# Weight tiles split once per layer and kept in DRAM, the normalised rows of the half that is used again kept there too, and six buffers of weight pairs

## The chip, the cores and the metric

The kernel runs on one core of one Trainium2 chip. Its metric is the device time of one launch in microseconds. Five engines work side by side, each through its own queue in order: TensorE (PE; its weight loads are PEld), VectorE (DVE), ScalarE (ACT), GpSimd (POOL) and SyncE (SP). SP only issues DMAs, and all of the kernel's own DMAs are issued there.

## The reference

An encoder trunk of two layers over two sequences of 1024 rows by 1024 columns, all in float32. Cut to what matters here, a layer is:

```
mod = silu(c) @ w_ada + b_ada;  shift, scale, gate = split(mod)
h    = rms_norm(x, g_pre) * (1 + scale) + shift
proj = h @ w_in                                  # 1024 x 4024, laid out as 32 tiles of 128 columns
mixed = concat(attention, rwkv7, mamba2, gated_deltanet)(proj)   # groups A, B, C, D, 256 wide each
x    = x + gate * rms_norm(mixed @ w_out, g_post)
```

Both sequences use the same `w_in` and `w_out` in a layer. Columns of `proj` feed the four head groups; B and D hold a scan in each direction, C a chunked scan, A an attention over all 1024 rows.

## The kernel before

A unit is one sequence in one layer; there are four, in the order (layer 0, sequence 0), (0, 1), (1, 0), (1, 1). Work on a unit has three parts: the input projection, the mixers, the output projection.

**Precision by splitting.** A projection multiplies float32 operands as pairs: `a = ah + al`, where `ah` is a rounded copy in the matmul's fast format and `al` the rest, and it sums `ah·bh`, `al·bh` and `ah·bl`. Rows `h` are held as `hh`, `hl`, weights as `wh`, `wl`. `split_w` makes a weight pair out of a loaded tile `w` of 128x512: ACT casts (line 327), DVE subtracts (line 329). Both are marked urgent, so the scheduler puts them ahead of the mixers' work on their queues.

**Input projection.** `stage_in` works on one half of a sequence, 512 rows, at a time. `norm_in` (lines 274 to 299) loads the rows, normalises them, transposes them on PE (line 294) and writes `hh` and `hl`; there is one buffer of each, 2 MB each. `in_tile` then goes through the weight tiles: two loads of 256 KB, two splits, 24 matmuls 128x512 through `paced` (line 458), one copy out of PSUM, one store to the tensor `P` in DRAM. The tiles for groups D and C of both halves come first, then the rest, so that a half is visited again after the other has overwritten `hh` and `hl`, and `norm_in` runs again on it: on both halves in unit 0, on the first half in the others. `norm_in` runs 13 times in all: four in unit 0, three in each other unit. A weight tile is loaded and split again for each half of each unit, 512 times for `w_in` and 128 times for `w_out` (`out_tiles`).

**Order.** A scheduler places every instruction by priority and simulated time. `spread`, `behind` and `ahead` give projection tiles priorities that are spread over the mixers' stretch, so that the projections' matmuls fill PE beside the scans; `paced` chains every few of them (TK, TO) through a memset of a token on POOL (line 462), which keeps them from running away. Buffers order the rest: `w` has two, `wh` and `wl` three each (GB, GL), the copy out of PSUM (`st`) three.

Of the kernel before, what the change touches and what calls it, by code (L numbers as in the profile page):

```python
# [10 lines left out]
F32 = mybir.dt.float32  # L11
F32R = mybir.dt.float32r
# [7 lines left out]
MUL, ADD, SUB = ALU.mult, ALU.add, ALU.subtract  # L20
# [1 line left out]
D = 1024  # L22
MIX = 1800
EA = 60
GK = 4
GB = 3
EB = 60
TK = 5
TO = 8
ED = 90  # L30
GL = 3
SB = 3
NPT = 8
EC = 60
T = 1024
DEPTH = 2
# [10 lines left out]
NWT = len(W_TILES)  # L47
W_D = ['sm', 'qkv0', 'qkv1', 'qkv2', 'qkv3', 'qkv4', 'qkv5']
W_B = ['xbc0', 'xbc1', 'xbc2', 'xbc3', 'xbc4', 'xbc5']
W_REST = ['zc0', 'zc1', 'zd0', 'zd1', 'wa', 'rkv0', 'rkv2', 'rkv4', 'rkv1', 'rkv3', 'rkv5', 'cq0', 'cq1', 'cq2', 'ckv', 'zb0', 'zb1', 'za0', 'za1']  # L50
W_ORDER = W_D + W_B + W_REST
# [57 lines left out]
class Body:  # L109
    def __init__(self, ctx, tc, A, outs, sl=None):  # L110
        self.tc, self.nc, self.A, self.outs = tc, tc.nc, A, outs
        self.n = 0
        self.side = "left"
        self.span = None
        nc = tc.nc
        self.cp = ctx.enter_context(tc.tile_pool(name="cp", bufs=1))
        self.dr = ctx.enter_context(tc.tile_pool(name="dr", bufs=1, space=DRAM))
        self.banks = 3
        self.held = None
        self.token = self.t(self.cp, [1, 1], tag="token")  # L120
        self.gate, self.run = None, 0
        self.ident = self.const(self.cp, "ident")
        self.blk = self.const(self.cp, "blk")
        self.bsel = self.const(self.cp, "bsel")
        self.cc = self.t(self.cp, [128, 4], tag="cc")
        nc.vector.memset(self.cc[:, 0:1], -0.5)
        nc.vector.memset(self.cc[:, 1:2], EPS)
        nc.vector.memset(self.cc[:, 2:3], 0.5)
        nc.vector.memset(self.cc[:, 3:4], 1.0)
        self.mhalf, self.eps, self.phalf, self.one1 = (self.cc[:, i:i + 1] for i in range(4))  # L130
# [127 lines left out]
                    for j in range(2):  # L258
                        nc.vector.tensor_scalar(L.gsc[:, k0 + j, :], ps2[:, 2 * j:2 * j + 2], 1.0, L.pp("gpre", k0 + j), ADD, MUL)

    def stage_in(self, s, L, l, xsrc, Pd, parts=((0, W_ORDER), (1, W_ORDER))):

        for hf, names in parts:
            if self.held is None or self.held[0] != (Pd, hf):
                self.spread()
                hh = self.t(self.pj, [128, 8, 512], F32R, tag="hh")
                hl = self.t(self.pj, [128, 8, 512], F32R, tag="hl")
                self.norm_in(s, L, xsrc, hf, hh, hl)
                self.held = (Pd, hf), hh, hl
            for name in names:  # L270
                self.spread()
                self.in_tile(l, name, hf, *self.held[1:], Pd)

    def norm_in(self, s, L, xsrc, hf, hh, hl):
            nc, pj, sp = self.nc, self.pj, self.sp
# [25 lines left out]
    def in_tile(self, l, name, hf, hh, hl, Pd):  # L301
        nc, pj = self.nc, self.pj
        ci = W_TILES.index(name)
        M = 88 if name == "sm" else 128
        ps = self.t(self.pps, [128, 512], tag="pj")
        for k in range(8):
            if k % 4 == 0:
                w = self.t(pj, [128, 4, 128], tag="w", bufs=2)
                self.dma(w, self.A["w_in"][l, ci][:, k * 128:k * 128 + 512].rearrange("p (k c) -> p k c", k=4))
            if k % GK == 0:  # L310
                with self.urgent():
                    wh, wl = self.split_w(w[:, k % 4:k % 4 + GK], [128, GK, 128])
            for i, (a, b) in enumerate(((wh, hh), (wh, hl), (wl, hh))):
                self.paced(TK, ps[0:M], a[:, k % GK, 0:M], b[:, k, :], dict(start=(k == 0 and i == 0), stop=(k == 7 and i == 2)))
        st = self.t(pj, [128, 512], tag="st", bufs=SB)
        with self.urgent():
            if name[0] == "z":
                nc.scalar.activation(st, ps, AF.Tanh, scale=0.5)
                nc.vector.scalar_tensor_tensor(st, st, 1.0, ps, ADD, MUL)
            else:  # L320
                nc.scalar.copy(st[0:M], ps[0:M])
        self.dma(Pd[ci * 128:ci * 128 + M, hf * 512:(hf + 1) * 512], st[0:M])

    def split_w(self, w, shape):
        nc, pj = self.nc, self.pj
        wh = self.t(pj, shape, F32R, tag="wh", bufs=GB)
        nc.scalar.copy(wh, w)  # L327
        wl = self.t(pj, shape, F32R, tag="wl", bufs=GL)
        nc.vector.tensor_tensor(wl, w, wh.bitcast(F32), SUB)  # L329
        return wh, wl  # L330

    def out_tiles(self, l, ch, hh, hl, kqs, at=lambda kq: kq):

        nc, pj = self.nc, self.pj
        pss = [self.t(self.pps, [128, 2, 256], tag="pj") for _ in range(2)]
        for n, kq in enumerate(kqs):
            w = self.t(pj, [128, 2, 256], tag="w", bufs=2)
            self.dma(w, self.A["w_out"][l, ch, kq // 2][:, (kq % 2) * 512:(kq % 2) * 512 + 512].rearrange("p (k c) -> p k c", k=2))
            with self.urgent():
                wh, wl = self.split_w(w, [128, 2, 256])  # L340
            for i in range(4):
                ps = pss[i // 2][:, i % 2]
                c = slice(i * 128, (i + 1) * 128)
                for k in range(2):
                    a, b = hh[:, at(kq) * 2 + k, c], hl[:, at(kq) * 2 + k, c]
                    first, last = n == 0 and k == 0 and i % 2 == 0, n == len(kqs) - 1 and k == 1
                    for m, (u, w2) in enumerate(((a, wh), (a, wl), (b, wh))):
                        self.paced(TO, ps, u, w2[:, k], dict(start=first and m == 0, stop=last and m == 2, skip_group_check=True))
        return pss

    def stage_out(self, s, L, l, xsrc, od, dst):
# [3 lines left out]
        for hf in range(2):  # L355
# [1249 lines left out]
    def full(self):  # L1605
        A = self.A
        x = [A["x0"], A["x1"]]
        L = [self.layer_params(l) for l in range(DEPTH)]
        P = {}
# [4 lines left out]
        def src(s, l):  # L1614
            return x[s] if l == 0 else x1[s]

        def run_in(u, *parts):
            s, l = units[u]
            if u not in P:
                P[u] = self.t(self.dr, [NWT * 128, 1024], tag="P", bufs=2)  # L1620
            self.stage_in(s, L[l], l, src(s, l), P[u], parts)

        def run_out(u):
            s, l = units[u]
# [20 lines left out]
        def out_last(parts, ctx=None):  # L1645
            s, l = units[3]
            self.stage_out_last(s, L[l], l, src(s, l), o[3], self.outs[s], parts, ctx)

        early = (0, W_D + W_B), (1, W_D + W_B)
        late = (1, W_REST), (0, W_REST)  # L1650
        with ExitStack() as io:
# [62 lines left out]

# [12 lines left out]
```

## Time and profile before

| | before |
|---|---|
| median of three runs | 4856.7 us (4849.28 to 4880.52) |
| the profiled execution's own time | 4863.89 us |
| its span | 4862.1 us |
| PE / PEld / DVE / ACT / POOL busy | 89% / 67% / 69% / 45% / 8% |
| mean granted TensorE clock | 0.877 |
| moved by DMA | 671.79 MB, 138 GB/s |

The profile is of one execution. Busy time counts an engine's instructions, not its waits; a wait is put down to the instruction that ended it. The chain of waits goes back from the last instruction to what released it, and its shares add up to the span.

### The profile page before, as it was taken

To read this page: it belongs to the slowest core of one execution; us is meant where nothing else is said; L and a number is where in the kernel's file an instruction comes from. 1 tells how busy PE (TensorE), PEld (TensorE's weight loads), DVE (VectorE), ACT (ScalarE), POOL (GpSimd) and SP (SyncE) were. 2 spreads that over 40 slices of the span, in tenths; PEclk is the share of its full clock that TensorE was granted. 3 is DMA by queue.
4 is the path that set the end of the run, shared out by engine and by line. 5 is a ranking of instruction groups with operands and counts; after the bars stand their busy time and mean duration, and the time that the engine had idled before them with its cause. 6 is when DMAs were issued, how large, how long until landed. Compare 5 with 4: busy or idle time off the path is not lost.

```text
span 4862.1 us, 100716 instructions
## 1 busy us (share of the span) xinstructions
PE 4303.3 (89%) x38644; PEld 3243.0 (67%) x38644; DVE 3351.1 (69%) x6837; ACT 2177.4 (45%) x4734; POOL 399.5 (8%) x2093
## 2 busy tenths in 40 slices
PE   6879798999898988998989898898989988889985
PEld 3657565767676775764767666775767766767675
DVE  2488878567688886555549869767556969857466
ACT  2444364554435453531554454454445254446233
POOL 0111010000101110000011100000011100000000
PEclk8889898998998897988989799797989988878688
DMA  4444364343543455453445354644245345365233
GB/s 146 136 146 143 99 196 145 100 114 117 164 148 121 144 162 158 129 152 100 138 144 164 113 166 132 197 140 135 70 149 177 129 135 157 111 200 146 75 100 127
DMA packets 495063, 671.79 MB, mean 138 GB/s; under 512 B 149752, under 2 KB 265976, under 8 KB 493560
## 3 DMA queue, kind: packets, MB, share of 16 engines
q1 hardware_dynamic: 494584, 665.36, 43.9%
q8 instruction: 306, 5.01, 0.4%
q14 instruction: 173, 1.42, 0.1%
HBM read 486.53 MB, written 178.57 MB: 137 GB/s over the span
## 4 chain that ended last, share of the span: by engine, by line
PE 58%; DVE 16%; DMA 14%; issue 5%; ACT 5%; SPq 1%; POOL 1%; DVEq 0%; POOLq 0%; ACTq 0%
PE pj L458 27%; PE b L824 2%; DVE iA L522 2%; PE b L1570 2%; PE b L551 2%; DMA w<-w_in 2%; PE pj L243 2%; PE b L557 1%; PE b L1557 1%; DVE wl L329 1%; DVE GT L537 1%; SPq L144 1%; PE y L1222 1%; PE b L1526 1%; PE b L590 1%
## 5 line engine op out<-in xcount | busy, mean ns | idle before, releaser
L458 PE MATMUL pj<-hh,wl 128*128 128x512 f32 (+1 forms) x2048 | 849.4, 415 | 41.9 <-DVE wl L329 28.8
L458 PE MATMUL pj<-hh,wh 128*128 128x512 f32 (+1 forms) x2048 | 854.2, 418 | 25.8 <-POOL token L462 10.2
L458 PE MATMUL pj<-hl,wh 128*128 128x512 f32 (+1 forms) x2048 | 847.4, 414 | 18.3 <-POOL token L462 18.2
L327 ACT CAST wh<-w 128x512 fp32r<-128x512 f32 x640 | 395.6, 618 | 782.6 <-PE pj L458 523.8
L329 DVE TENSOR_TENSOR wl<-w,wh 128x512 fp32r<-128x512 f32 x640 | 447.3, 700 | 253.3 <-ACT wh L327 211.7
L458 PEld LDWEIGHTS pj<-hh,wl 128*128 128x128 f32 (+1 forms) x2048 | 397.2, 194 | 148.1 <-DVE wl L329 27.6
L458 PEld LDWEIGHTS pj<-hh,wh 128*128 128x128 f32 (+1 forms) x2048 | 398.0, 194 | 128.8 <-POOL token L462 16.1
L458 PEld LDWEIGHTS pj<-hl,wh 128*128 128x128 f32 (+1 forms) x2048 | 397.8, 194 | 113.9 <-POOL token L462 26.3
L462 POOL MEMSET token<- 1x1 f32 x1613 | 143.4, 89 | 3347.0 <-PE pj L458 3342.1
L458 PE MATMUL pj<-wh,hl 128*128 128x256 f32 x896 | 270.7, 313 | 1.3 <-DVE hl L363 1.2
L1561 ACT ACTIVATE pT<-b 128x512 f32<-128x512 f32 x256 | 150.7, 598 | 262.7 <-PE b L1559 258.2
L458 PE MATMUL pj<-wh,hh 128*128 128x256 f32 x768 | 236.2, 308 | 11.5 <-ACT st L372 5.9
L458 PE MATMUL pj<-wl,hh 128*128 128x256 f32 x768 | 231.5, 302 | 3.7 <-DVE wl L329 3.7
L294 PE MATMUL pj<-c_ident,x 128*128 128x128 f32 x416 | 120.4, 393 | 122.0 <-DVE x L289 43.9
L1527 DVE TENSOR_REDUCE mx<-b 128x1 f32<-128x512 f32 x256 | 169.9, 684 | 84.1 <-PE b L1526 82.4
L638 DVE SCALAR_TENSOR_TENSOR cva<-cvi,cw,cva 128x1024 f32<-128x1024 f32 x144 | 183.7, 1278 | 46.8 <-ACT cva L634 33.8
L458 PEld LDWEIGHTS pj<-wh,hl 128*128 128x128 f32 x896 | 182.8, 208 | 17.5 <-issue 9.7
L1570 PEld LDWEIGHTS b<-VO,pT 128*64 128x64 f32 x4096 | 152.8, 144 | 52.1 <-issue 43.9
L1570 PE MATMUL b<-VO,pT 128*64 128x65 f32 x4096 | 182.5, 233 | 0.9 <-ACT pT L1561 0.9
L824 PE MATMUL b<-AR,BK 64*64 64x128 f32 x2048 | 178.4, 305 | 3.5 <-DVE G L829 3.2
L829 DVE SCALAR_TENSOR_TENSOR G<-b,Dk,mk 128x128 f32<-128x128 f32 x512 | 140.7, 341 | 53.2 <-PE b L824 52.8
L296 ACT ACTIVATE ht<-pj,shc,gsc 128x256 f32<-128x256 f32 x208 | 118.6, 570 | 126.8 <-PE pj L294 63.2
(403 smaller groups left out, 9125.1 us busy)
## 6 DMA issues: line engine op xcount, KB each, us to landing
w<-w_in SPq DMA_DIRECT2D x512, 256.0 KB
P<-st SPq DMA_DIRECT2D x248, 256.0 KB
x<-x SPq DMA_DIRECT2D x76, 512.0 KB
w<-w_out SPq DMA_DIRECT2D x128, 256.0 KB
G<-P SPq DMA_DIRECT2D x112, 256.5 KB
cvi<-P SPq DMA_DIRECT2D x48, 512.0 KB
f<-acr SPq DMA_DIRECT2D x32, 512.0 KB
bkc<-bkd SPq DMA_DIRECT2D x64, 256.0 KB
```

The lines of the kernel that those rows point to most:

```text
L294: nc.tensor.transpose(ps[:, i * 128:(i + 1) * 128], xs[i][:, k * 128:(k + 1) * 128], self.ident)
L296: nc.scalar.activation(ht, ps[:, 0:256], AF.Identity, scale=L.gsc[:, k, s:s + 1], bias=L.shc[:, k, s:s + 1])
L327: nc.scalar.copy(wh, w)
L329: nc.vector.tensor_tensor(wl, w, wh.bitcast(F32), SUB)
L458: m = self.nc.tensor.matmul(*mm[:3], **mm[3]).ins
L462: t = self.nc.gpsimd.memset(self.token, 0.0).ins
L638: nc.vector.scalar_tensor_tensor(a, c[:, j:j + 1024], wt(j, i), a, MUL, ADD)
L824: nc.tensor.matmul(pss[x][self.half(x ^ a), i * 128:i * 128 + 128], BK[self.half(x), pr, c, a], AR[self.half(x), pr, c].rearrange("p a t - ...
L829: v.scalar_tensor_tensor(G[:, x, pr, c, :], pss[x][:, i * 128:i * 128 + 128], Dk[:, c, 2 * x + pr:2 * x + pr + 1], mk, MUL, MUL)
L1527: v.tensor_reduce(mx[:, n, qt:qt + 1], ps, AX.X, ALU.max, negate=True)
L1561: nc.scalar.activation(pT[kt], ps, AF.Exp)
L1570: nc.tensor.matmul(po[64 * x:64 * x + 64, i, :], pT[kt][:, o:o + 64], VO[:, kt, h, :], start=(kt == 0 and i == 0), stop=(kt == 7), skip_gr ...
```

## The change

`split_w` gives way to `halves`. On the first use of a tile in a layer it loads `w`, splits it into the two halves of one 4 KB wide buffer `w2`, and stores the pair, 512 KB, into a tensor in DRAM. On each later use of the same tile (the other half, the other sequence) it loads the pair from there, 512 KB, and splits nothing. `w2` has six buffers; `wh` and `wl` are gone. The first `norm_in` of a half that will be visited again (five of them, the set `twice`) also stores `hh` and `hl`, 2 MB each, and the second visit loads them in place of running `norm_in`. The setting `dynamic_dma_scratch_size` goes from its default to 1024.

```diff
 def stage_in(...):
...
-                self.norm_in(s, L, xsrc, hf, hh, hl)
+                back = self.spilled.get((s, l, hf))
+                if back is None:
+                    self.norm_in(s, L, xsrc, hf, hh, hl)
+                    if again[n]:
+                        self.spilled[s, l, hf] = back = self.t(self.dr, [2, 128, 4096], tag="hd", bufs=2)
+                        for i, h in enumerate((hh, hl)):
+                            self.dma(back[i], h.bitcast(F32).rearrange("p k t -> p (k t)"))
+                else:
+                    for i, h in enumerate((hh, hl)):
+                        self.dma(h.bitcast(F32).rearrange("p k t -> p (k t)"), back[i])
...
 def in_tile(...):
-                w = self.t(pj, [128, 4, 128], tag="w", bufs=2)
-                self.dma(w, self.A["w_in"][l, ci][:, k * 128:k * 128 + 512].rearrange("p (k c) -> p k c", k=4))
-            if k % GK == 0:
-                with self.urgent():
-                    wh, wl = self.split_w(w[:, k % 4:k % 4 + GK], [128, GK, 128])
+                w2 = self.halves(("in", l, ci, k // 4), lambda: self.A["w_in"][l, ci][:, k * 128:k * 128 + 512]).rearrange("p u (k c) -> p u k c", k=4)
...
-    def split_w(self, w, shape):
+    def halves(self, key, src):
+
         nc, pj = self.nc, self.pj
-        wh = self.t(pj, shape, F32R, tag="wh", bufs=GB)
-        nc.scalar.copy(wh, w)
-        wl = self.t(pj, shape, F32R, tag="wl", bufs=GL)
-        nc.vector.tensor_tensor(wl, w, wh.bitcast(F32), SUB)
-        return wh, wl
+        w2 = self.t(pj, [128, 2, 512], F32R, tag="w2", bufs=WB)
+        wf = w2.bitcast(F32)
+        if key in self.kept:
+            self.dma(wf, self.kept[key])
+            return w2
+        w = self.t(pj, [128, 512], tag="w", bufs=2)
+        self.dma(w, src())
+        with self.urgent():
+            nc.scalar.copy(w2[:, 0], w)
+            nc.vector.tensor_tensor(w2[:, 1], w, wf[:, 0], SUB)
+        kept = self.wd[key[:2]]
+        self.kept[key] = kept[key[2] * 2 + key[3]] if key[0] == "in" else kept[key[2] * 4 + key[3]]
+        self.dma(self.kept[key], wf)
+        return w2
...
+        twice = {(0, 0), (0, 1), (1, 0), (2, 0), (3, 0)}
...
-    nc = bacc.Bacc("TRN2", target_bir_lowering=False, num_devices=1)
+    nc = bacc.Bacc("TRN2", target_bir_lowering=False, num_devices=1, dynamic_dma_scratch_size=1024)
```

`out_tiles` takes its pairs from `halves` in the same way. The scheduler orders the whole program anew. Three places show what that does.

VectorE in the last unit, in the forward inversion of group D (`SC`, `iT`: lines 529 and 530 before, 543 and 544 after). Before:

```order
L530 TENSOR_TENSOR SC_40582<-SC_40582,iT_40588 128x18x14
L329 TENSOR_TENSOR wl_38869<-w_38865,wh_38867 128x512
L529 TENSOR_TENSOR iT_40588<-SC_40582,iA_40587 128x247
L1335 TENSOR_TENSOR f_42697<-cb_6930_42687,f_42697 128x512
L1335 TENSOR_TENSOR f_42697<-cb_6931_42692,f_42697 128x512
L530 TENSOR_TENSOR SC_40582<-SC_40582,iT_40588 128x19x13
L329 TENSOR_TENSOR wl_38889<-w_38885,wh_38887 128x512
L529 TENSOR_TENSOR iT_40588<-SC_40582,iA_40587 128x240
L530 TENSOR_TENSOR SC_40582<-SC_40582,iT_40588 128x20x12
```

Now:

```order
L544 TENSOR_TENSOR SC_38143<-SC_38143,iT_38149 128x18x14
L543 TENSOR_TENSOR iT_38149<-SC_38143,iA_38148 128x247
L544 TENSOR_TENSOR SC_38143<-SC_38143,iT_38149 128x19x13
L543 TENSOR_TENSOR iT_38149<-SC_38143,iA_38148 128x240
L544 TENSOR_TENSOR SC_38143<-SC_38143,iT_38149 128x20x12
L1364 SCALAR_TENSOR_TENSOR y_40137<-xt_39810,rp_17_105,yd_40214 128x8x64
L1356 TENSOR_TENSOR xd_40269<-xt_39810,dt_39812 128x1024
L543 TENSOR_TENSOR iT_38149<-SC_38143,iA_38148 128x231
```

The subtractions of line 329 that stood between the steps of the inversion are gone from this stretch.

TensorE in unit 0, where the projection comes back to the first half (`hh_768` to `hh_1500` before, `hh_775` to `hh_1454` now). Before, its start and its end:

```order
L458 MATMUL pj_1456<-hh_768,wl_1481 128x512
L571 MATMUL b_4189<-c_ident_61,cva_4180 128x128 x4
L571 MATMUL b_4200<-c_ident_61,cva_4180 128x128 x4
L1066 MATMUL b_4228<-KQ_3816 64x128 x8
L1066 MATMUL b_4238<-KQ_3816 64x128 x8
L1066 MATMUL b_4248<-KQ_3816 64x128 x7
L294 MATMUL pj_1520<-c_ident_61,x_1502 128x128
L294 MATMUL pj_1527<-c_ident_61,x_1502 128x128
...
L294 MATMUL pj_1643<-c_ident_61,x_1585 128x128
L458 MATMUL pj_1650<-hh_1500,wh_1653 128x512
```

Now:

```order
L472 MATMUL pj_1410<-hh_775,w_271_1431 128x512
L604 MATMUL b_3537<-cc_71,cvt_3532 64x1 x32
L585 MATMUL b_3583<-c_ident_65,cva_3527 128x128 x4
L585 MATMUL b_3594<-c_ident_65,cva_3527 128x128 x4
L585 MATMUL b_3617<-c_ident_65,cva_3608 128x128 x4
L585 MATMUL b_3628<-c_ident_65,cva_3608 128x128 x4
L472 MATMUL pj_1458<-hh_1454,w_277_1459 128x512
L472 MATMUL pj_1458<-hl_1455,w_277_1459 128x512
```

The 32 transposes are gone, and 48 instructions of the mixers stand between the last matmul on the old rows and the first on the reloaded ones. At the other four returns 122, 40, 56 and 42 stand there.

SyncE at the same return. Before:

```order
L144 DMA f_854_4222<-gcr_3791 64x2048 x2
L144 DMA x_1576<-x 128x1024
L144 DMA x_1585<-x 128x1024
L144 DMA x_2780<-x 128x1024
L144 DMA x_2789<-x 128x1024
L144 DMA w_1761<-w_in 128x512
```

Now (a `w_` with a second number is a buffer `w2`, `win` the pairs in DRAM):

```order
L145 DMA w_1432<-w_in 128x512
L145 DMA win_1_60<-w_269_1411 128x1024
L145 DMA w_1681<-w_in 128x512
L145 DMA w_277_1459<-win_1_60 128x1024
...
L145 DMA w_285_1533<-win_1_60 128x1024
L145 DMA hl_1455<-hd_458 128x4096
L145 DMA hh_1454<-hd_458 128x4096
L145 DMA P_307<-st_1451 128x512
L145 DMA w_286_1549<-win_1_60 128x1024
L145 DMA kvd_3256<-kv_3582 64x4x64 x4
```

The reload's two DMAs of 2 MB stand ahead of the next store to `P` and of small stores of group D; a store of a split pair stands ahead of the next tile's load.

## Rows read from the trace of the kernel before

**Rows 1.** The page: engines, DMA queue, and the chain that ended last.
```profile
PE 4303.3 (89%) x38644; PEld 3243.0 (67%) x38644; DVE 3351.1 (69%) x6837; ACT 2177.4 (45%) x4734; POOL 399.5 (8%) x2093
...
q1 hardware_dynamic: 494584, 665.36, 43.9%
...
PE 58%; DVE 16%; DMA 14%; issue 5%; ACT 5%; SPq 1%; POOL 1%; DVEq 0%; POOLq 0%; ACTq 0%
PE pj L458 27%; PE b L824 2%; DVE iA L522 2%; PE b L1570 2%; PE b L551 2%; DMA w<-w_in 2%; PE pj L243 2%; PE b L557 1%; PE b L1557 1%; DVE wl L329 1%; DVE GT L537 1%; SPq L144 1%; PE y L1222 1%; PE b L1526 1%; PE b L590 1%
```

**Rows 2.** Windows, four stretches: length, busy per engine (count), clock, DMA share, GB/s.
```profile
243.00:851.00 608.00, 527.24 (x4295) 390.12 (x4296) 500.42 (x987) 293.80 (x612) 63.39 (x300) 0.89 0.47 145
...
3768.00:4254.00 486.00, 433.74 (x3893) 346.40 (x3891) 403.81 (x821) 213.12 (x487) 46.20 (x258) 0.88 0.42 133
sum 2067.00, PE 1829.85 PEld 1417.15 DVE 1732.70 ACT 954.25 POOL 215.01; mean PE 457.46 PEld 354.29 DVE 433.18 ACT 238.56 POOL 53.75
```

**Rows 3.** The same four windows, line 329 alone.
```profile
sum 2067.00, DVE 249.70; mean DVE 62.42
```

**Rows 4.** Groups by line: shapes, count, busy us, mean ns, idle before, what ended it.
```profile
L458 PE MATMUL pj<-hh,wl 128*128 128x512 f32 (+1 forms) x2048 | 849.4, 415 | 41.9 <-DVE wl L329 28.8
...
L327 ACT CAST wh<-w 128x512 fp32r<-128x512 f32 x640 | 395.6, 618 | 782.6 <-PE pj L458 523.8
L329 DVE TENSOR_TENSOR wl<-w,wh 128x512 fp32r<-128x512 f32 x640 | 447.3, 700 | 253.3 <-ACT wh L327 211.7
```

**Rows 5.** Chain by line, in tenths of a per cent (the whole span).
```profile
by line: PE pj L458 27.1%; issue 4.8%; PE b L824 2.2%; DVE iA L522 2.2%; PE b L1570 2.0%; PE b L551 1.8%; DMA w<-w_in 1.8%; PE pj L243 1.8%; PE b L557 1.4%; PE b L1557 1.3%; DVE wl L329 1.3%; DVE GT L537 1.3%; SPq L144 1.3%; PE y L1222 1.2%
```

**Rows 6.** DMA issues: count and KB each.
```profile
w<-w_in SPq DMA_DIRECT2D x512, 256.0 KB
...
w<-w_out SPq DMA_DIRECT2D x128, 256.0 KB
...
cq<-P SPq DMA_DIRECT2D x8, 1024.0 KB
```

**Rows 7.** Chain in order of time, some DMA pieces: start, us, what.
```profile
337.98 4.28 DMA w<-w_in
...
683.54 5.38 DMA P<-st
688.93 3.60 DMA G<-P
...
753.82 8.82 DMA cq<-P
...
1322.21 10.41 DMA w<-w_in
```

**Rows 8.** Windows, the five returns to a normalised half.
```profile
262.00:300.00 38.00, 20.66 (x170) 14.22 (x170) 24.26 (x37) 21.50 (x42) 4.21 (x8) 0.69 0.49 126
526.00:575.00 49.00, 25.56 (x108) 16.51 (x107) 43.25 (x95) 22.89 (x47) 4.76 (x16) 0.65 0.20 68
1490.00:1535.00 45.00, 31.29 (x328) 23.76 (x327) 40.03 (x100) 30.94 (x79) 5.92 (x6) 0.65 0.34 115
...
3930.00:3960.00 30.00, 25.86 (x243) 18.14 (x244) 17.27 (x51) 21.13 (x57) 1.58 (x7) 0.83 0.28 92
sum 202.00, PE 139.76 PEld 99.72 DVE 148.98 ACT 125.47 POOL 17.92; mean PE 27.95 PEld 19.94 DVE 29.80 ACT 25.09 POOL 3.58
```

**Rows 9.** Groups by line: `norm_in`'s transposes and its first write.
```profile
L294 PE MATMUL pj<-c_ident,x 128*128 128x128 f32 x416 | 120.4, 393 | 122.0 <-DVE x L289 43.9
...
L296 ACT ACTIVATE ht<-pj,shc,gsc 128x256 f32<-128x256 f32 x208 | 118.6, 570 | 126.8 <-PE pj L294 63.2
```

**Rows 10.** What SyncE's queue waited for: us in total, times, longest.
```profile
SPq L144 <- DVE wl L329: 580.7, 232, 23.2
SPq L144 <- ACT st L321: 307.8, 129, 8.2
...
SPq L144 <- DMA P<-st: 72.6, 41, 4.8
```

More of the change, by code (lines that the diff above doesn't have):

```diff
@@ L24 @@
 EA = 60
-GK = 4
-GB = 3
 EB = 60
@@ L30 @@
 ED = 90
-GL = 3
 SB = 3
+WB = 6
 NPT = 8
@@ L119, in __init__ @@
         self.held = None
+        self.kept = {}
+        self.wd = {(n, l): self.t(self.dr, [m, 128, 2, 512], tag=f"w{n}{l}") for l in range(DEPTH) for n, m in (("in", 2 * NWT), ("out", 16))}
+        self.spilled = {}
         self.token = self.t(self.cp, [1, 1], tag="token")
@@ L259, in ada, with stage_in @@
                         nc.vector.tensor_scalar(L.gsc[:, k0 + j, :], ps2[:, 2 * j:2 * j + 2], 1.0, L.pp("gpre", k0 + j), ADD, MUL)
-    def stage_in(self, s, L, l, xsrc, Pd, parts=((0, W_ORDER), (1, W_ORDER))):
-        for hf, names in parts:
+    def stage_in(self, s, L, l, xsrc, Pd, parts, again):
+        for n, (hf, names) in enumerate(parts):
             if self.held is None or self.held[0] != (Pd, hf):
@@ L307, in in_tile @@
             if k % 4 == 0:
-                w = self.t(pj, [128, 4, 128], tag="w", bufs=2)
-                self.dma(w, self.A["w_in"][l, ci][:, k * 128:k * 128 + 512].rearrange("p (k c) -> p k c", k=4))
-            if k % GK == 0:
-                with self.urgent():
-                    wh, wl = self.split_w(w[:, k % 4:k % 4 + GK], [128, GK, 128])
-            for i, (a, b) in enumerate(((wh, hh), (wh, hl), (wl, hh))):
-                self.paced(TK, ps[0:M], a[:, k % GK, 0:M], b[:, k, :], dict(start=(k == 0 and i == 0), stop=(k == 7 and i == 2)))
+                w2 = self.halves(("in", l, ci, k // 4), lambda: self.A["w_in"][l, ci][:, k * 128:k * 128 + 512]).rearrange("p u (k c) -> p u k c", k=4)
+            for i, (a, b) in enumerate(((0, hh), (0, hl), (1, hh))):
+                self.paced(TK, ps[0:M], w2[:, a, k % 4, 0:M], b[:, k, :], dict(start=(k == 0 and i == 0), stop=(k == 7 and i == 2)))
         st = self.t(pj, [128, 512], tag="st", bufs=SB)
@@ L336, in out_tiles @@
         for n, kq in enumerate(kqs):
[L337 to L340, printed above, removed]
+            w2 = self.halves(("out", l, ch, kq), lambda: self.A["w_out"][l, ch, kq // 2][:, (kq % 2) * 512:(kq % 2) * 512 + 512]).rearrange("p u (k c) -> p u k c", k=2)
             for i in range(4):
@@ L346, in out_tiles @@
                     first, last = n == 0 and k == 0 and i % 2 == 0, n == len(kqs) - 1 and k == 1
-                    for m, (u, w2) in enumerate(((a, wh), (a, wl), (b, wh))):
-                        self.paced(TO, ps, u, w2[:, k], dict(start=first and m == 0, stop=last and m == 2, skip_group_check=True))
+                    for m, (u, x) in enumerate(((a, 0), (a, 1), (b, 0))):
+                        self.paced(TO, ps, u, w2[:, x, k], dict(start=first and m == 0, stop=last and m == 2, skip_group_check=True))
         return pss
@@ L1620, in run_in @@
                 P[u] = self.t(self.dr, [NWT * 128, 1024], tag="P", bufs=2)
-            self.stage_in(s, L[l], l, src(s, l), P[u], parts)
+            self.stage_in(s, L[l], l, src(s, l), P[u], parts, [(u, hf) in twice and names[0] == W_D[0] for hf, names in parts])
         def run_out(u):
```

## The prediction

> **What bounds the kernel now.** I read the page first, then windows over stages, then waits and the chain. The page shows no engine that is full [rows 1]: PE 89%, DVE 69%, ACT 45%, and a chain that is 58% PE, 16% DVE, 14% DMA, 5% ACT. The windows show where DVE comes near to PE [rows 2]: in four stretches, 2067 us together, PE is busy 1830 us and DVE 1733; in these the projections run beside the inversions of D. So PE has the most work, and what it waits for changes from place to place; PE was idle 4862 - 4303 = 559 us in all. No engine's saved time can be booked in full.
>
> The splits take part in three ways. They cost 396 us of ACT and 447 us of DVE. PE itself hardly waits for them: 28.8 us before a matmul for `wl` [rows 4]. But the queues stand still for them: DVE idles 212 us because the next in its queue is a subtraction whose cast is not done, and ACT idles 524 us because the next is a cast whose buffer a projection matmul still reads [rows 4]. On the chain they are small: `wl` 1.3% (63 us), the wait for a weight load 1.8% (88 us) [rows 5].
>
> **The change, part by part.** The profiled execution took 4863.9 us, span 4862.1; it is 7 us above the median of the runs shown, 4856.7.
>
> *Splits.* 640 become 160 (in each layer 64 for `w_in` and 16 for `w_out`). That takes away 480 x 0.618 = 297 us of ACT and 480 x 0.700 = 336 us of DVE [rows 4]. On the path: three quarters of the chain's 63 us, -47. For ACT no row gives the casts' share of the chain; ACT's 5% of the chain is 243 us out of 2177 busy, 11%, and 11% of 297 is 33; the other end is nothing. I take -20, since a cast mostly stands in the queue early.
>
> *Queues that stand still less.* Three quarters of DVE's 212 us go: between 0 and -159, on top. No row tells whether work was waiting behind it; PE ran the projection meanwhile, so I take a quarter, -40.
>
> *Weight loads.* A tile needs 512 KB in place of 256 [rows 6], but there are six buffers in place of two. The wait of 88 us could go (-88) or, if each stays on the path, grow. The queue moved 665.36 MB in 43.9% of the span, 2134 us [rows 1], so 312 GB/s while busy; 256 KB more are 0.84 us beside a load's 4.28 [rows 7], a fifth: +18. I take -30: the six buffers hold 5 x 12 matmuls of work ahead, at 0.415 us each [rows 4] some 25 us or, since they overlap, half of that; both exceed most waits for a load [rows 7].
>
> *Normalised rows.* Five of the 13 `norm_in` go: 160 transposes, 180 ACT and 120 DVE instructions. In the five stretches where they stood, PE was idle 202 - 140 = 62 us [rows 8], and the transposes cost 120.4 x 5/13 = 46 us more of busy time [rows 9]. In their place PE needs two reloads of 2 MB. At 312 GB/s these take 13.4 us; by the row of a 1024 KB load, 8.82 us, 35 us [rows 6, 7]. Only 40 to 122 mixer instructions stand there on PE as cover (the order shows it), perhaps 10 to 25 us. The stall of the projection stream is thus 13 to 35 us where it was 30 to 40 by the lengths of the stretches [rows 8]. Ends: -108 with full cover, and five times 35 - 10 = 25 us of idle, 125 - 108 = +17. I take 15 us of idle in each, 75 in all, as a reload at 312 GB/s with a little queue and little cover gives, and so -30 in round numbers. What the clock gives back in these stretches (granted 0.65 and 0.69 in unit 0 [rows 8], between its two levels of 1.2 and 2.4 GHz) I don't book: a PE that waits for a reload is as idle as one that waits for `norm_in`.
>
> *Everything else that moves by DMA.* The bytes: 160 loads of 256 KB, 160 stores and 480 loads of 512 KB, less 640 loads of 256 KB: +210 MB; five times 8 MB for the rows, less five times 2 MB of `x`: +31 MB. So 665 becomes 906 MB, and the share of 43.9% becomes 60%, in the four dense stretches from 0.42 to 0.47 [rows 2] to some 0.65. The DMAs on the chain other than weight loads are 14% - 1.8%, 593 us; by pieces of 3.6 to 5.4 us [rows 7], about 150. Ends: 0, and +0.36 x 593 = +214 if they lengthen with the load. I take +60, 0.4 us a piece, half the 0.84 us that a further 256 KB in front would cost. SP's queue is the only one. Its wait for subtractions, 581 us, was for the `w` buffers [rows 10]; now it waits for matmuls to free `w2`, and each first use adds a store that waits for its subtraction, with the next load, stores to `P` and the scans' small DMAs behind it. The 73 us that SP waited for an earlier store to land [rows 10] will grow; in the +60.
>
> *The scratch.* All DMAs are issued by SP in hardware-generated form [rows 1]; nothing in the page uses the scratch: 0.
>
> Sum: -47 - 20 - 40 - 30 - 30 + 60 = -107; 4864 - 107 = 4757, and 7 less on the scale of the median: **4750 us**, -2.2%.
>
> **The rivals.**
>
> *More: DVE was the bound in the dense stretches.* For it: DVE is 84% busy there, in order, with 250 us of it spent on splits [rows 3]. Three quarters of these are 187 us, and PE has 237 us of idle to give [rows 2]. Against it: PE is at 89% in the same stretches. If the 187 us go in full, with -30 and -30 for loads and rows and +60 for DMA, 4857 - 187 = 4670; without the DMA cost 4610.
>
> *Nothing: PE's work sets the time.* PE keeps all but 160 of its matmuls and transposes, and the projection's tokens keep their pace. If the mixers' relief ends in PE's queue and the DMAs cost what the loads gain, what is left is the row term: 4830 to 4857.
>
> *Slower: the single DMA queue.* The mechanism is one queue with 2 MB reloads and 512 KB pairs in front of the scans' small DMAs. Price: one pair ahead of each chain DMA is 1.68 us; 150 x 1.68 = +252, less the 167 of gains, is 4857 + 85 = 4942. It decides from 1.1 us per chain DMA (167/150) on. For it: chain pieces already range up to 8.82 and 10.41 us [rows 7], and a piece of the chain has no slack by its nature. Against it: at 60% the DMA engines still idle, and the pairs are asked for early.
>
> A rule of the Trainium skill speaks for this rival ("DMA: Bandwidth & Descriptors", section Latency and other measured facts): it gives the access to device memory as 0.2 us on average and 2 us at high load. By it 1.8 us on each of 150 pieces would be +270 and the time about 4960, an estimate; no row here shows memory at such a load.
>
> *The change does not do what it says.* The order shows 160 splits left and 480 pair loads; so only the buffers could fail, if pairs come late; that is inside the slower case.
>
> **How the numbers follow.** My forecast, between 4660 and 4808: 0.48. More (under 4660): 0.14. Nothing (within 1%, which is about what a measurement of this kernel can tell from no change; 4808 to 4905): 0.20. Slower (over 4905): 0.18. So faster 0.62, same 0.20, slower 0.18. The forecast's own range is 4660 to 4808. For 8 in 10 the range goes down to 4620, leaving 0.08 of the larger gains, and up to 4930, leaving 0.12 of the slower case.
>
> **What would show it.** Right: ACT busy below 1790 us (297 and 160 x 0.570 = 91 less [rows 9]) and DVE below 3015 (336 less); `wl` gone from the chain's first lines; PE's share of the span up to 90% or more, with a busy time some 50 us less; 906 MB and a DMA share near 60%. The reload: in the five places an idle PE of 10 us or less. Wrong by the DMA term: chain DMA above 17%, with pieces of the scans (`kvd`, `UV`, `bkc`, `qf`) 1 us longer, and SP waiting for landings hundreds of us. Wrong by the bound: DVE's share falls, PE's stays at 89% and the stretches are as long as before.

## The result and the profile after

| | before | after |
|---|---|---|
| median of four runs each, same chip | 4854.32 us (4849.28 to 4880.52) | 4731.18 us (4724.56 to 4735.23) |
| ratio, 95% interval | | 0.9735 [0.9704, 0.9766] |
| span of the profiled execution | 4862.1 us | 4722.7 us |
| PE / DVE / ACT busy | 4303 / 3351 / 2177 us | 4205 / 3014 / 1818 us |
| mean granted TensorE clock | 0.877 | 0.892 |
| moved on the kernel's queue | 665 MB, 43.9% | 907 MB, 59.9% |

The change is 123 us faster, -2.65%; forecast were 4750 us and -2.2%. The page of the changed kernel answers to [rows 1]: engines, queue, and the chain that ended last.

```profile
PE 4204.5 (89%) x38484; PEld 3184.7 (67%) x38484; DVE 3013.8 (64%) x6237; ACT 1817.7 (38%) x4054; POOL 381.8 (8%) x2073
...
q1 hardware_dynamic: 517624, 906.54, 59.9%
...
PE 4%; DVE 1%; DMA 1%; ACT 0%; issue 0%; SPq 0%; POOL 0%; POOLq 0%; DVEq 0%; ACTq 0%
```

The last line must be read with care: its shares add up to some 6%, so the chain was lost soon after the end of the span and says nothing of the other 94%. The chain of this kernel cannot be set beside that of [rows 1, 5].

The 139 us of span are 99 us less of busy PE (4303.3 to 4204.5) and 41 us less of idle PE (559 to 518). Groups by line, in the form of [rows 4, 9] (count, busy us, mean ns, idle before and what ended it):

```profile
L472 PE MATMUL pj<-hh,w 128*128 128x512 f32 (+1 forms) x4096 | 1431.1, 420 | 61.0 <-POOL token L476 27.6 <-DMA hh<-hd 11.2 <-DVE st L326 8.5
...
L343 DVE TENSOR_TENSOR w<-w,w 128x512 fp32r<-128x512 f32 x160 | 113.5, 710 | 121.2 <-ACT w L342 118.2 <-DMA cvi<-P 1.3 <-PE pj L472 1.2
...
L342 ACT CAST w<-w 128x512 fp32r<-128x512 f32 x160 | 98.9, 620 | 247.6 <-DMA w<-w_in 173.8 <-PE pj L472 43.6 <-DMA w<-w_out 15.3
...
L305 PE MATMUL pj<-c_ident,x 128*128 128x128 f32 x256 | 75.7, 400 | 61.0 <-DVE ss L297 33.2 <-ACT hh L309 20.2 <-DVE x L300 7.1
```

The transposes (line 305) account for 45 of the 99 us, and their idle time halved (122.0 to 61.0). The other 54 us are the same matmuls in less time, at a granted clock of 0.892 where it was 0.877. The projection's wait for a reloaded half is in the first row: 11.2 us. DVE's idle time in front of a subtraction fell from 212 us to 118, ACT's in front of a cast from 524 (for a buffer) to 44.

The places where a half comes back, in windows as long as those of [rows 8] (the fourth 45 us where it was 40), and the tile `hd` itself:

```profile
254.00:292.00 38.00, 27.66 (x206) 22.66 (x207) 17.90 (x24) 8.97 (x11) 6.75 (x16) 0.82 0.92 301
...
1469.00:1514.00 45.00, 28.64 (x320) 25.03 (x320) 42.11 (x60) 5.52 (x9) 7.20 (x15) 0.75 0.59 212
...
sum 207.00, PE 167.52 PEld 132.16 DVE 123.16 ACT 58.08 POOL 17.23; mean PE 33.50 PEld 26.43 DVE 24.63 ACT 11.62 POOL 3.45
```

```profile
who waited for it (us, times):
  PE pj L472: 11.2, 3
```

PE is idle 39 us in these five windows, 62 before; two of the reloads held up no matmul at all, the first, at a DMA share of 0.92, one for 0.9 us, the third one for 7.9 us and the fifth one for 2.3 us.

The dense stretches of [rows 2], between the same counts of the mixers' matmuls (the first and the last of the four), and line 343 alone in them, as in [rows 3]:

```profile
267.00:856.00 589.00, 528.00 (x4287) 404.34 (x4287) 424.16 (x852) 218.40 (x473) 54.96 (x300) 0.86 0.66 214
3720.00:4194.00 474.00, 429.61 (x3920) 337.72 (x3919) 365.32 (x732) 159.31 (x388) 46.79 (x268) 0.93 0.65 210
```

```profile
267.00:856.00 589.00, 27.93 (x38) 0.86 0.66 214
3720.00:4194.00 474.00, 10.93 (x16) 0.93 0.65 210
```

DVE fell from 82 and 83% to 72 and 77% there, but the stretches only went from 608 to 589 and from 486 to 474 us: DVE's relief became DVE's idle time. These two stretches give 31 of the 139 us. Windows cut where the mixers of a unit end, before and then after (PE, PEld, DVE, ACT, POOL busy, clock, DMA share, GB/s):

```profile
0.00:1274.00 1274.00, 1118.72 (x9636) 813.54 (x9636) 851.77 (x1772) 600.76 (x1231) 109.51 (x572) 0.90 0.43 134
1274.00:2486.00 1212.00, 1080.94 (x9572) 787.87 (x9570) 819.86 (x1688) 513.79 (x1149) 93.24 (x468) 0.87 0.45 140
2486.00:3633.00 1147.00, 1032.27 (x9550) 790.62 (x9548) 823.94 (x1674) 539.11 (x1173) 99.70 (x522) 0.89 0.46 142
3633.00:4862.00 1229.00, 1071.32 (x9892) 850.98 (x9891) 855.53 (x1703) 523.73 (x1182) 97.02 (x531) 0.85 0.44 136
```

```profile
0.00:1297.00 1297.00, 1145.05 (x9630) 831.00 (x9630) 760.22 (x1622) 498.39 (x1049) 100.09 (x562) 0.88 0.60 198
1297.00:2430.00 1133.00, 1015.00 (x9486) 751.90 (x9483) 747.51 (x1552) 439.48 (x999) 92.72 (x467) 0.90 0.61 195
2430.00:3591.00 1161.00, 1041.92 (x9516) 798.17 (x9516) 744.67 (x1528) 453.42 (x1010) 95.00 (x517) 0.88 0.60 191
3591.00:4722.00 1131.00, 1002.57 (x9859) 803.60 (x9859) 761.43 (x1535) 426.38 (x997) 93.96 (x527) 0.91 0.61 189
```

The parts went by +23, -79, +14 and -98 us, although DVE is relieved by 72 to 94 us in each. A gain of busy time on DVE does not turn into span in proportion; where the span fell, the clock rose (0.87 to 0.90, 0.85 to 0.91), and where it grew, the clock fell (0.90 to 0.88, 0.89 to 0.88).

SyncE's queue, in the form of [rows 10], and the DMA issues, as [rows 6]:

```profile
SPq L145 <- PE pj L472: 945.9, 413, 14.3
SPq L145 <- DVE w L343: 130.7, 61, 6.0
SPq L145 <- PE pj L305: 126.4, 13, 25.5
SPq L145 <- ACT st L328: 122.2, 115, 7.6
...
SPq L145 <- DMA P<-st: 72.7, 38, 4.8
```

```profile
w<-win SPq DMA_DIRECT2D x384, 512.0 KB
win<-w SPq DMA_DIRECT2D x128, 512.0 KB
```

The queue that stood for subtractions (581 us) and copies (308 us) now stands for matmuls that free a `w2` (946 us). It does not stand longer for stores to `P` to land (72.7 us where it was 72.6), nor for DMAs of all kinds to land (252 us where it was 251).

### The profile page after: what moved, and what is told of

It is laid out like the page before. It is cut to its first block, busy times and chain, and to the rows that moved or that the text cites. A ratio compares the mean times of both kernels' runs of the same rounds, so it can differ in the third digit from the quotient of the medians.

```text
span 4722.7 us, 98675 instructions
## 1 busy us (share of the span) xinstructions
PE 4204.5 (89%) x38484; PEld 3184.7 (67%) x38484; DVE 3013.8 (64%) x6237; ACT 1817.7 (38%) x4054; POOL 381.8 (8%) x2073
## 3 DMA queue, kind: packets, MB, share of 16 engines
q1 hardware_dynamic: 517624, 906.54, 59.9%
## 5 line engine op out<-in xcount | busy, mean ns | idle before, releaser
L472 PE MATMUL pj<-hh,w 128*128 128x512 f32 (+1 forms) x4096 | 1431.1, 420 | 61.0 <-POOL token L476 27.6
L472 PEld LDWEIGHTS pj<-hh,w 128*128 128x128 f32 (+1 forms) x4096 | 785.0, 195 | 268.1 <-issue 40.8
L472 PE MATMUL pj<-hl,w 128*128 128x512 f32 (+1 forms) x2048 | 856.4, 418 | 16.5 <-POOL token L476 16.2
L472 PEld LDWEIGHTS pj<-hl,w 128*128 128x128 f32 (+1 forms) x2048 | 399.7, 195 | 116.3 <-POOL token L476 25.2
L472 PE MATMUL pj<-w,hh 128*128 128x256 f32 x1536 | 334.5, 308 | 9.3 <-POOL token L476 6.0
L472 PEld LDWEIGHTS pj<-w,hh 128*128 128x128 f32 x1536 | 261.6, 204 | 32.2 <-issue 9.4
L472 PE MATMUL pj<-w,hl 128*128 128x256 f32 x960 | 267.0, 305 | 0.2 <-DVE hl L377 0.2
L472 PEld LDWEIGHTS pj<-w,hl 128*128 128x128 f32 x960 | 185.2, 203 | 11.6 <-issue 3.6
L1219 ACT ACTIVATE SE<-SC,el 64x64 f32<-64x64 f32 x480 | 141.1, 338 | 117.9 <-DVE SC L1230 59.7
L838 PEld LDWEIGHTS b<-AR,BK 64*64 64x64 f32 x2048 | 115.3, 155 | 46.7 <-issue 37.4
```

The source lines that it names most:

```text
L472: m = self.nc.tensor.matmul(*mm[:3], **mm[3]).ins
L838: nc.tensor.matmul(pss[x][self.half(x ^ a), i * 128:i * 128 + 128], BK[self.half(x), pr, c, a], AR[self.half(x), pr, c].rearrange("p a t - ...
L1219: nc.scalar.activation(SE[half(x), pr], VS[half(x), x, pr, i, :], AF.Identity, scale=el[half(x), d, pr, c:c + 1])
```

## The experiments

Two theories stood at the start. **Sum**: the parts add up as the prediction has them. **Order**: the scheduler places the whole program anew for every edit, and a good part of the 2.65% is the order that the spreads of 60 happened to give. Each run stands beside runs of the kernel before on its own chip; these had medians of 4869.58, 4868.27 and 4871.02 us, where the first chip had 4854.32, so up to 17 us of a difference between two chips is the chip's.

### The parts alone

Splits kept in DRAM, rows not:

```diff
-        twice = {(0, 0), (0, 1), (1, 0), (2, 0), (3, 0)}
+        twice = set()
```

> The change without the kept rows: tiles are split once and kept, norm_in runs 13 times as before. Theory (sum of the prediction's terms): splits -67, queues -40, weight loads -30, DMA +52 of the 60, so 4854 - 85 = about 4770. Rival 'rows': most of the gain came from the five norm_in that went, since PE lost 46 us of transposes and idled 62 us there; then 4820 or more here. Rival 'DVE was the bound': nearly the whole gain or more is here, 4740 or less.

Measured: 4949.02 us, ratio 1.0145 [1.0107, 1.0183]. DVE is relieved by 280 us and ACT by 264, and the kernel is 79 us slower. **Sum** had some 4770 us here. The rival 'rows' covers the number with its "4820 or more", but it expected a smaller gain and not a loss.

Rows kept in DRAM, on the kernel before, with its 640 splits:

```diff
-                self.norm_in(s, L, xsrc, hf, hh, hl)
+                back = self.spilled.get((s, l, hf))
...
+                        self.dma(h.bitcast(F32).rearrange("p k t -> p (k t)"), back[i])
```

> The kernel before with the rows kept alone: hh and hl of five halves are stored and reloaded, weights are split 640 times as before. Theory: -30 for the rows, +8 for their DMAs, about 4832. Rival 'rows': 4770 or less, by 46 us of transposes and up to 62 us of idle PE. If the two parts add up, this gain and that of the splits alone make the 123 us of the whole change; less means that they share one resource, more that each covers the other's cost.

Measured: 4837.45 us, 0.9921 [0.9892, 0.9951], -32 us. **Sum** had about 4832.

Six buffers of pairs and the small scratch, with a split at every use and nothing kept:

```diff
-        if key in self.kept:
-            self.dma(wf, self.kept[key])
-            return w2
...
-        self.dma(self.kept[key], wf)
...
+        twice = set()
```

> The kernel before with the pair buffers of the change alone (six w2 in place of three wh and three wl, scratch 1024): each tile is loaded and split every time, nothing is kept in DRAM, norm_in runs 13 times. Theory: only part of the weight-load and queue terms, at most -40, so 4815 to 4855. Rival 'buffers': the wait of ACT's casts for a buffer that a matmul still reads (524 us of idle) was what held the mixers, and the deeper buffers alone give most of the gain: 4770 or less.

Measured: 4833.88 us, 0.9931 [0.9895, 0.9967], -36 us. So keeping the pairs, on top of the six buffers, costs 115 us where rows are not kept, and keeping the rows, on top of that, brings some 200 (the ratios go from 1.0145 to 0.9735, 4.1%). The parts do not add up: -36 of the buffers and -32 of the rows are near what was expected of them, the rest is an interaction.

PE in the profiles of the six buffers alone and then of the splits alone:

```profile
PE 4248.7 (88%) x38644; PEld 3212.0 (66%) x38644; DVE 3343.9 (69%) x6837; ACT 2174.2 (45%) x4734; POOL 401.9 (8%) x2093
```

```profile
PE 4367.5 (88%) x38644; PEld 3263.4 (66%) x38644; DVE 3071.2 (62%) x6357; ACT 1913.7 (39%) x4254; POOL 396.9 (8%) x2093
```

Neither the -36 nor the +115 us is idle time of PE. The spans are 4830.9 and 4953.7 us, so PE is idle 582 us with the six buffers, 586 with the splits and 559 in the kernel before. It is the same 38644 matmuls that take 4249, 4367 and 4303 us, at a mean granted clock of 0.886, 0.872 and 0.877.

### What the transfers cost

480 copies of 512 KB from DRAM to DRAM, on the same queue, one behind the load of each later use of a pair:

```diff
         if key in self.kept:
             self.dma(wf, self.kept[key])
+            self.dma(self.t(self.dr, [128, 2, 512], tag="xx", bufs=8), self.kept[key])
             return w2
```

> The change with a DRAM to DRAM copy of 512 KB beside each of the 480 pair loads, read by nobody: 252 MB more on the same queue, as much as the change itself added, and 480 more DMAs for SP to issue. Theory (0.4 us for each DMA on the chain): +60 to +100 on 4731, so 4790 to 4830. Slower rival (single queue): +200 or more, 4930 on. If DMA had been free all along: 4745 or less, and the +60 of the sum was wrong.

Measured: 5254.95 us, 1.0785 [1.0733, 1.0837]. The loss is not spread out. Two stretches of this kernel, and what PE waited for in the first:

```profile
487.00:833.00 346.00, 185.74 (x1428) 140.63 (x1425) 126.19 (x254) 64.25 (x168) 15.42 (x104) 0.73 0.99 339
2891.00:3310.00 419.00, 195.28 (x1450) 150.93 (x1449) 134.78 (x254) 60.67 (x155) 17.14 (x105) 0.69 0.95 322
```

```profile
PE pj L473 <- DMA w<-win: 94.9, 10, 36.1
```

```profile
PE pj L473 <- DMA w<-win: 122.0, 7, 99.1
```

The last row is the same wait in the second stretch. In these 765 us PE is busy 381; at the 89% of the whole change its work would have taken 428 us, so some 340 of the 520 us lost to the change stand here, where the DMA share is 0.95 and 0.99. Elsewhere the share is 0.61 to 0.81. But the copies are not spread out either: 313 of the 480 are issued in these two stretches. By this estimate a copy costs 1.1 us inside (340/313) and 1.1 us outside (180/167), so the run does not show that a transfer is cheaper at the lower share.

The expectation of 0.4 us a piece (+60 to +100) fails, and that of the slower rival (+200 or more) holds. How much of the loss is the run's own is not shown: its copies share eight buffers in DRAM, and SyncE stood 361 us for an earlier copy to land, with everything else behind.

### The splits' engine time, on top of the change

An urgent cast and a subtraction into unused tiles at each of the 480 later uses:

```diff
             self.dma(wf, self.kept[key])
+            with self.urgent():
+                ja = self.t(pj, [128, 512], BF16, tag="ja")
+                nc.scalar.copy(ja, wf[:, 0])
+                jb = self.t(pj, [128, 512], BF16, tag="jb")
+                nc.vector.tensor_tensor(jb, wf[:, 0], ja, SUB)
             return w2
```

> The change with a cast on ACT and a subtraction on DVE, both urgent, added at each of the 480 later uses of a tile; they read the loaded pair and write tiles that nobody reads. So ACT and DVE do nearly all their old work again, while PE waits for loads alone. Theory (terms of the sum): the 47, 20 and 40 us of splits and standing queues come back, about 4838. Rival 'DVE was the bound': +187 or more, 4918. If engine time and queues never mattered and the gain is the rows' and the buffers': 4750 or less.

Measured: 4905.99 us, 1.0081 [1.0048, 1.0113] to the kernel before, some 170 us above the change (3.5%, by the ratios). The groups of the added work:

```profile
L342 DVE TENSOR_TENSOR jb<-w,ja 128x512 bf16<-128x512 f32 x480 | 335.0, 698 | 336.8 <-ACT ja L340 334.4
L340 ACT CAST ja<-w 128x512 bf16<-128x512 f32 x480 | 296.4, 617 | 675.7 <-DMA w<-win 403.3 <-DVE jb L342 132.6 <-DMA w<-wout 105.8
```

The durations are those of real splits (0.698 and 0.617 us), but ACT now stands 509 us for pairs to land and DVE 334 us for ACT. **Sum** had 4838 us and is 68 short; the rival 'DVE was the bound' had 4918 or more and is nearly met. That doesn't bear it out, since the run prices splits together with longer waits for loads than real ones have (ACT's in front of a cast were 180 us in the kernel before). It does not tell the 631 us of busy time from those waits, and the order differs as well; no price of the busy time alone comes from it.

### Another order, nothing else

The spreads EA, EB, EC at 55 in place of 60, in the splits alone, the change and the kernel before:

```diff
-EA = 60
+EA = 55
...
-EB = 60
+EB = 55
...
-EC = 60
+EC = 55
```

> Splits kept alone, as in e1_splits_only, with another spread of the projections over the mixers (EA, EB, EC 55 in place of 60), which gives another order of the whole program. Theory 'order': the 80 us that the splits alone lost in e1 are one order's bad luck, and a like change of the spread moves the time by 1 to 2%: 4780 to 4870 here. Rival 'norm_in is in the way': splits without kept rows lose in any order, because norm_in's loads wait at the head of SP's queue in front of the pairs: 4920 or more again.

> The whole change with the same other spread (55). If the order alone moves a kernel by 1 to 2%, this lies anywhere between 4690 and 4800; if the change is robust, within 1% of 4731. It must stay below the other two of this spread (splits alone, and before) if the gain is the change's own and not the order's.

> The kernel before with the same other spread (55): the control for the two with 55. If the order is worth 1 to 2%, 4800 to 4950; if it is worth nothing, 4840 to 4870.

Measured: splits alone 4869.17 us, the change 4766.31, the kernel before 4779.90, against 4868.27 for the kernel before at 60. A number that adds or removes no work moved the kernel before by 1.9% (0.981 [0.9786, 0.9835]), as much as most of the edits above. At 55 the change and the kernel before stand 14 us apart, with an interval that holds no change (0.9974 [0.9943, 1.0004], worked out from the runs). That spoke for **order**, although the change stayed within 1% of 4731 as a robust change should, and the kernel before fell below both of its expected ranges. But splits alone lose here too, 89 us to the kernel before at 55, ratio 1.0186 [1.0156, 1.0215]: that loss came in both orders tried.

The same edit with 50 and with 65, in the change and in the kernel before:

> The changed kernel with the spreads of the projection tiles, EA, EB, EC, at 50 in place of 60; nothing else differs. At 60 the change stood 2.65% under the kernel before, at 55 only 0.3% (4766 against 4780 us). Theory 'most of the 2.65% is the order that 60 happened to give': the mean difference of change and before over several spreads is near 1%, and at 50 this kernel stands between 4740 and 4830 us, within 1.5% of the kernel before with the same spread. Rival 'the change is worth 2 to 3% by itself and 55 was a lucky order of the kernel before alone': this kernel stands 2 to 3% under the kernel before with the same spread, wherever that lies. If less of the spread leaves the projections too late, both kernels rise together, over 4850.

> The kernel before with spreads of 50. Theory 'order': it may land anywhere between 4770 and 4900 us, since 60 to 55 alone moved it by 1.9%, and its distance to the change at 50 is 0 to 1.5%. Rival 'own gain': 2 to 3% over the change at 50.

> The changed kernel with spreads of 65. Theory 'order': 4720 to 4830 us and, against the kernel before with 65, a difference that is not that of 60 (-2.65%) nor of 55 (-0.3%) but anywhere from +0.5 to -3%. Rival 'own gain': 2 to 3% under the kernel before with 65.

> The kernel before with spreads of 65. Theory 'order': 4770 to 4900 us, with no smooth line through 50, 55, 60 and 65. Rival 'own gain': 2 to 3% over the change at 65, and 50, 60 and 65 alike within half a per cent, with 55 alone out of line.

| spread | before | the change | difference | ratio |
|---|---|---|---|---|
| 50 | 4892.81 | 4796.95 | -96 | 0.9797 [0.9750, 0.9844] |
| 55 | 4779.90 | 4766.31 | -14 | 0.9974 [0.9943, 1.0004] |
| 60 (first chip) | 4854.32 | 4731.18 | -123 | 0.9735 [0.9704, 0.9766] |
| 65 | 4876.88 | 4750.10 | -127 | 0.9745 [0.9712, 0.9777] |

The intervals of 50, 55 and 65 are worked out from the runs of both kernels. **Order** expected a mean difference near 1%, and it falls: in three of four orders the change gives 2 to 2.7%, and the mean of the four is -90 us, -1.9%. Four orders that lie between -0.3 and -2.65% fix that mean only roughly. The rival ("55 is a lucky order of the kernel before alone") did better: on the chip that ran 50 and 65, the kernel before stands at 4892.81, 4871.02 and 4876.88 us with 50, 60 and 65, within half a per cent as it had put it, and 55 alone is out of line. Over the four orders, on three chips, the change moves by 66 us, the kernel before by 113. No order tried beats the change as it stands.

### Why the splits alone lose

At 60 the whole loss lies in unit 0. The four parts, cut where the mixers of a unit end as above, went by +91, -5, +11 and -6 us. The first of them, with the splits alone:

```profile
0.00:1365.00 1365.00, 1179.38 (x9615) 844.36 (x9616) 778.26 (x1657) 537.35 (x1114) 110.42 (x569) 0.87 0.55 173
```

In it one stretch stands out, between the same counts of the mixers' matmuls, and it does so at 55 too. Before and splits alone, at 60 and then at 55; each time the stretch and SyncE's wait for `norm_in`'s transposes in it:

```profile
795.00:1168.00 373.00, 348.95 (x3504) 252.61 (x3502) 254.58 (x526) 189.21 (x377) 16.63 (x125) 0.95 0.37 110
```

```profile
SPq L144 <- PE pj L294: 41.0, 4, 19.5
```

```profile
811.00:1253.00 442.00, 404.19 (x3555) 286.24 (x3553) 248.80 (x537) 174.61 (x352) 19.54 (x130) 0.86 0.40 121
```

```profile
SPq L145 <- PE pj L305: 76.0, 3, 50.5
```

```profile
802.00:1188.00 386.00, 365.15 (x3543) 263.76 (x3540) 250.66 (x518) 189.39 (x376) 16.56 (x128) 0.93 0.37 108
```

```profile
SPq L144 <- PE pj L294: 26.1, 3, 14.7
```

```profile
807.00:1237.00 430.00, 394.70 (x3527) 276.44 (x3524) 250.96 (x527) 175.80 (x351) 17.94 (x129) 0.87 0.40 121
```

```profile
SPq L145 <- PE pj L305: 79.9, 5, 36.6
```

The stretch is 69 and 44 us longer, out of 92 and 94 us of span. Near the end a second one is longer by 50 us (60) and 58 us (55), but there PE has 249 and 430 more matmuls: work that came later, and at 60 the last unit as a whole did not grow.

The first thought is the queue: SyncE stands up to 50.5 us for a row buffer that waits for transposes, and every pair that PE will need is behind it. The traces do not bear that out. With the splits alone no matmul of the whole run at 60 waited for a pair, and two did at 55, for 5.4 us in all. Only 14 of the 69 us, and 14 of the 44, are idle PE; 55 and 30 are busy PE, with nearly the same number of matmuls, at a granted clock of 0.86 and 0.87 where it was 0.95 and 0.93. Below is the place where the clock fell at 60. The first row is all work in 80 us, the second the projection's matmuls among it; the third is all work in the like piece of the kernel before:

```profile
1131.00:1211.00 80.00, 77.28 (x488) 49.38 (x487) 31.55 (x84) 24.21 (x47) 3.75 (x7) 0.59 0.08 24
```

```profile
1131.00:1211.00 80.00, 0.87 (x3) 0.57 (x3) 0.59 0.08 24
```

```profile
1070.00:1110.00 40.00, 40.00 (x454) 26.35 (x453) 21.86 (x60) 20.00 (x40) 2.64 (x6) 1.00 0.16 53
```

While `norm_in` prepares the next half, PE has all but 3 of its matmuls there from the mixers and the transposes. It runs them almost without a pause, and from 1138 us on the same matmuls take longer (start, us, what, number):

```profile
1137.55 0.44 PE L838 MATMUL b<-AR,BK 64*64 64x128 f32 x2
1138.33 0.68 PE L838 MATMUL b<-AR,BK 64*64 64x128 f32 x2
```

SyncE's 50.5 us fall into these 80: the transposes that it waits for come a few at a time between the mixers' matmuls on a slow PE, and PE itself waited only 2.7 us there. In the kernel before PE ran the like, with ten projection matmuls among them, for 40 us at a clock of 1.00. Why this piece got longer with kept pairs, and why the clock fell in it, is not shown.

Over the whole span SyncE's waits for these transposes are 178 to 244 us in the seven kernels of this study that run `norm_in` 13 times, whatever their order, and 95 to 130 us in the seven that run it eight times. With splits alone they are 227 us, with the six buffers 207 and in the kernel before 220, so their sum does not tell the kernel that lost from those that did not. That the rows are worth 32 us beside splits and some 200 (60) and 103 us (55) beside kept pairs is measured. That the kept rows help by taking `norm_in`, and the stretch without projection matmuls, out of these places fits the rows above; no run set the place of `norm_in` or of the reloads by itself, so it is argued, not shown.

## Why the prediction was right, step by step

**Direction and size** were right: -123 us against -107, and -90 over four orders. That the sum came so near is in part luck: too small a cost for the transfers stood against a gain on PE that it had no term for.

The chain of the changed kernel at 60 is lost. In the only kernel of the change whose chain was followed to its start, that at 65, the page gives the chain by engine:

```profile
PE 54%; DMA 18%; DVE 17%; ACT 4%; issue 4%; SPq 2%; POOL 1%; DVEq 0%; POOLq 0%; ACTq 0%
```

and some DMA pieces of it, in order of time (start, us, what):

```profile
831.68 8.07 DMA cq<-P
...
1426.02 13.32 DMA hh<-hd
...
3070.14 9.90 DMA cq<-P
...
3854.67 12.65 DMA hh<-hd
```

All pieces of this chain and of that of the kernel before, added up by what they are, in us, beside what the prediction had booked:

| pieces of the chain | before, 60 | change, 65 | difference | booked |
|---|---|---|---|---|
| subtractions of the splits | 63 | 27 | -36 | -47 |
| casts of the splits | 25 | 8 | -18 | -20 |
| loads of weights and pairs | 90 | 105 | +15 | -30 |
| reloads of rows | 0 | 26 | +26 | within the rows' -30 |
| other DMAs | 601 (150 pieces) | 746 (164) | +145 | +60 |
| PE | 2833 | 2561 | -272 | -46 for transposes, within the rows' -30 |

Each chain adds up to its span within 7 us. It is one execution of each, at two spreads, and a chain that leaves one engine goes on over another, so a difference is not a price; what the table leaves out rose by 29 us. But the directions are plain.

*Splits, -67, and queues, -40, with DMA +60*: on the chain of the change the splits gave 54 us, near what was booked. By themselves they did not: keeping the pairs over the six buffers measured +115 at 60, where these terms come to -47. The step that failed there is to book relieved engines and shorter queues as time of the path, with SyncE's new waits "in the +60". DVE and ACT had some 270 and 260 us less to do than with the six buffers, PE's idle time did not move (582 and 586 us), and its matmuls took 119 us longer. In the change the kept rows more than make up for this, so the error cancelled within the sum.

*Weight loads, -30, and scratch, 0*: the six buffers with the small scratch measured -36 at one order, but not by shorter waits, since PE's idle time rose by 23 us and its busy time fell by 55. On the chain the loads did not shrink. The number was met by luck; no run set the scratch by itself.

*Normalised rows, -30*: alone -32. But the working was wrong: it had 15 us of idle PE at each reload, 75 in all, and PE waited 11.2 us in three waits. The sign given, 10 us or less of idle per reload, holds for the mean (39/5 = 8 us) and just fails for the first (38 - 28 = 10.3 us); in the third window (16 us) half is the reload's. What was missed is that the rows' worth depends on the other half of the change.

*DMA, +60*: 150 pieces were counted on, and 150 there were. They got longer by 0.55 us on average (4.00 to 4.55), where 0.4 was booked, and there were 14 more. So the term was less than half of what the chain shows, and the sign "chain DMA above 17%" was met; the kernel was faster nonetheless, because PE's share fell by more. Of the scans' pieces that were to be 1 us longer, `UV` (3.6 to 5.3 us) and `SC<-kvd` (2.9 to 4.4) were, `bkc` (3.6 to 3.9) and `qf` (5.8 to 6.4) were not, by a few pieces of each. The 1024 KB loads of [rows 7] did not lengthen (8.82 us before; 8.07 and 9.90 here), and a reload of both tiles, 4 MB, took 13 us, as 312 GB/s had it.

The rule that spoke for the slower case, in the Trainium skill's "DMA: Bandwidth & Descriptors", section Latency and other measured facts, has 2 us of access to device memory at high load. At a DMA share of 0.6 no run shows 1.8 us more on each piece; the chain shows 0.55. At 0.99 PE's waits for a pair were 9.5 us on average and up to 36.1, at 0.95 17 us and up to 99.1, far over that figure; transfers queued ahead would explain that, and no run tells them apart.

*The rivals.* "More" did not come: DVE's share in the dense stretches fell and their length hardly did, by 19 and 12 us. "Nothing" described the first and third part of the run (+23, +14) but not the others. "Slower" has the number that the kept pairs give alone (4949 us; it had 4942), but by chance as far as is shown: beside the six buffers PE's idle time did not grow, while the rival wanted 1.7 us more on each DMA of the path, where the change has 0.55.

*The other signs.* DVE came to 3014 us (under 3015 was said), the queue to 906.54 MB and 59.9% (906 and 60%). PE's share stayed at 89%, where 90% or more was said, since busy and idle time fell alike; its busy time fell by 99, where 50 was said: 45 are the transposes, and the clock rose. ACT came to 1818, where under 1790 was said: the 480 casts gave 396 - 99 = 297 us as booked, but the busy count of the engine only fell by 360, as neighbours overlap in it.

**What stays open**: what the order at 55 has that the kernel before gains 1.9% by it, why kept pairs without kept rows cost PE its clock, and how the gain of the change divides between the shorter queues, the order and the clock. They differ together in every pair of runs, so none separates them.

## What to carry to other kernels

Where a scheduler orders the whole program by priorities, run each version at several harmless settings before a difference of 2% is put down to the edit: here one setting gave -0.3% and its neighbour -2.65%, and only four together gave -1.9%. Two halves of a change have to be tried apart and together: kept pairs lost 1.5 and 1.9%, kept rows gained 0.8%, both gave up to 2.7%. Bytes that seem to hide are not free: with 36% more of them SyncE waited no longer for landings, but the DMA pieces of the chain came to 876 us where they were 691. And when an engine is relieved, look for what PE does in the meantime before its time is booked as gain.

## What was not expected of the hardware

The two stretches at a DMA share of 0.95 and 0.99 moved 322 and 339 GB/s, per busy time 339 and 342, beside 312 GB/s that the queue moved while busy in the kernel before. So a share of 0.95 means that little is left.

The granted clock fell while PE was busy: 0.59 on average over 80 us in which PE ran small matmuls for 97% of the time by the profile, with the change to slower matmuls in the middle of an unbroken row of them; from 1151 to 1191 us it stood at 0.50, the lower of its two levels (1.2 GHz, where 1.00 is 2.4). It stood at 1.00 over 40 us of a like stretch of the kernel before; what decides between the two is not shown. Over whole runs the clock goes with the time, though not strictly: 0.892 at 4723 us of span, 0.886 at 4831, 0.877 at 4862 and 0.872 at 4954, but 0.875 at 4838 and 0.880 at 4895. A loss of this kind shows up as slower matmuls (55 of 69 us above), so a table of idle time alone misses it.
